# First layer of a two-layer streaming encoder: TensorE's order by a planner, and written out in pieces of three matmuls

## The chip, the cores and the metric

One core of one Trainium2 chip runs the whole program in one launch. The metric is device microseconds from the first to the last instruction of one execution; the median of three runs stands for a kernel. Engines are named as the profile names them: PE is TensorE (matmuls; PEld its weight loads), DVE VectorE, ACT ScalarE, POOL GpSimd, SP the engine that issues the transfers.

## The reference, cut to what matters

1024 prompt frames and 32 sample frames (T = 1056) of width 1024 go through two layers. The change lies in the first alone:

```python
def even_mixer(h, w_in, w_mix, scale, table, w_out, ...):
    proj = h @ w_in                              # 1024 -> 3072
    u, q, k, v, g_pool, g_att = split(proj)      # 512 columns each
    pool_out = multi_scale_pool(u, ...)          # 4 groups of 128, trailing means of 2, 4, 8, 16, minus u, times w_mix[g]
    att = band_attention(q, k, v, table)         # 8 heads of 64; own chunk of 64 frames and the 8 before, plus a bias
    mixed = concat([pool_out * silu(g_pool), att * silu(g_att)])
    return mixed @ w_out                         # then a norm and the residual
```

The 32 sample frames attend to 512 cached keys and values and to themselves. Layer two is an mLSTM with the same kind of projections.

## The kernel before, in words

**Layout.** Activations lie feature-major, tokens along the free axis, in three token groups (384, 384, 288: `GR`). A projection of 128 output columns ("a dense") reads one weight tile of 8 blocks of 128x128 and the normed input, both split into a high and a low part, so each block costs three matmuls (`mm3`, L106 to L108). One dense is 3 groups x 8 blocks x 3 = 72 matmuls. Each group goes to one of three PSUM buffers `pd` and is then evacuated by an `ev` function: by ACT for v (L248), by DVE for q and k (L256, L258), u (L612) and the gates (`gated`, L268 to L271, with a tanh on ACT between).

**Weights.** `take` hands out the weight tile that is asked for and loads the next one: a DMA, two casts on ACT (L93, tile `wh`), two subtractions on POOL (L94, tile `wl`). `wh` and `wl` have two buffers, so the next tile is split while the present one is multiplied, and its split can start only when the tile before is through.

**Layer 0** (`layer0`) works on four pairs of heads. The order in which the program is traced for each pair is: what was left of the fills; the transposes of v to token-major (`v_tokens`, L288 with ACT's L289 behind them); splits of q; the dense of k; its splits (`stacked`, `swapped`); the bias band B (DMA, a memset on POOL); the dense of the attention's gate, written into the tile `ga`, of which there is one; then the attention. `PLAN` names the denses put behind each pair (v and q of the next pair, u and gp of a pooling group): 4, 3, 3 and 4 of them, as fills.

**Attention.** A pair has two heads e and two halves hf of the 512 queries. `att_s(e, hf)` does the scores (L342, L343; 4 key blocks for hf 0, 8 for hf 1) in PSUM buffers `ps` (three), adds the bias (DVE L347, ACT L355), takes the maximum over the keys (DVE L363 to L371, then one `partition_all_reduce` on POOL, L373), subtracts it (DVE L377) and takes the exponential (ACT L378). `att_pv(e, hf)` multiplies by the values (L388, fp32, two instructions a block) into the one buffer `pv`, and `att_take` copies the result out (ACT L396, L397). `att_out` multiplies by the gate on POOL (L408), takes a reciprocal on DVE (L409) and stores to the DRAM tile `mix`. `att_sample` does the same for the 32 sample frames: its scores (L429, L430), an all-reduce of its own (L441), its exponential (L444), its values (L454) and a transpose (L459) in one function `rest`.

**Pooling.** `pool_sums` adds a group's windows on POOL (L477, one to four additions) and finishes on DVE (L481, L483); `pool_mix` multiplies by the mixing matrix (L495, one PSUM buffer `pm`) and by the gate gp (DVE L497).

**What sets the order.** The kernel is traced under Tile with `schedule_with_timeline_sim=True`: a planner runs a timing model over the traced program and, on each engine, places the instruction that is ready, earliest traced first. All engines then run their own list in order. So PE's list, too, is the planner's. After the four pairs, `out_proj` reads `mix` back in 384-token slices (`xr`, two buffers), splits them (ACT L195; POOL or DVE L196) into the tiles that the input had, and starts the output projection.

Of the kernel before, what the change touches and what calls it, by code (L numbers as in the profile page):

```python
# [15 lines left out]
DEC = 32  # L16
# [17 lines left out]
class Net:  # L34
# [36 lines left out]
    # keeps [s, t] with s <= t  # L71
# [4 lines left out]
    # ---------------------------------------------------------------- dense  # L76
# [40 lines left out]
    # the same, one token group at a time, to be put between other work; "make" gives evac when the tile starts  # L117
    def later(self, take, xs, make, after=None):
        box = {}

        def step(gi):
            if gi == 0:
                box["w"] = take()
                box["ev"] = make()
# [3 lines left out]
        self.fills += [lambda gi=gi: step(gi) for gi in range(3)]  # L128
# [15 lines left out]
    # r = 1/sqrt(sum/1024 + eps), on all partitions, from per-partition sums; worked out with the tokens on the partitions  # L144
# [44 lines left out]
    # split x * g into two parts of 12 bits  # L189
# [15 lines left out]
    # the input: one group's tokens, with tiles that are not in use yet for what comes in  # L205
# [23 lines left out]
    # ---------------------------------------------------------------- layer 0  # L229
# [32 lines left out]
    # (1 + tanh(g/2)) * g, twice the silu  # L262
# [11 lines left out]
    def v_tokens(self, vT, pr):  # L274
# [8 lines left out]
        for b0 in (0, 4, 8):  # L283
# [6 lines left out]
        for e in range(2):  # L290
            c0 = pr * 128 + e * 64
            cs = slice(e * 128, e * 128 + 64)
            nc.sync.dma_start(out=io["vo"][0:512, c0:c0 + 64].rearrange("(b p) c -> p b c", p=128), in_=vt[:, 4:8, cs])
            nc.sync.dma_start(out=io["vo"][512:544, c0:c0 + 64], in_=vt[:DEC, 8, cs])
        return vt

    # hi and lo of both heads, stacked on the partitions
# [21 lines left out]

    def att_s(self, pr, e, hf, Q, KA, KB, B):  # L320
# [7 lines left out]
        for group in banks:  # L328
            st = self.lp.tile([128, 1280], F32, name="st", bufs=4)
            tiles.append((st, [j for js in group for j in js]))  # L330
            off = 0
            for js in group:
# [28 lines left out]
        mx = self.lp.tile([128, 512], F32, name="mx", bufs=2)  # L361
        if hf == 0:
            nc.vector.tensor_copy(out=mx[:, 0:128], in_=place[0][0][:, 0:128])  # L363
            nc.vector.tensor_tensor(out=mx[:, 128:512], in0=place[0][0][:, 128:512], in1=place[1][0], op=ALU.max)
            rest = [2, 3]
        else:
            nc.vector.tensor_tensor(out=mx, in0=place[3][0], in1=place[4][0], op=ALU.max)
            rest = [2, 1, 0, 5, 6, 7]
        for j in rest:
            dst, a, b = place[j]  # L370
            nc.vector.tensor_tensor(out=mx[:, a - q0:b - q0], in0=mx[:, a - q0:b - q0], in1=dst, op=ALU.max)  # L371
        mb = self.lp.tile([128, 512], F32, name="mb", bufs=1)
        nc.gpsimd.partition_all_reduce(mb, mx, 128, bass_isa.ReduceOp.max)  # L373
        for st, js in tiles:
            for j in js:
                dst, a, b = place[j]
                nc.vector.tensor_tensor(out=dst, in0=dst, in1=mb[:, a - q0:b - q0], op=ALU.subtract)  # L377
            nc.scalar.activation(out=st, in_=st, func=AF.Exp)  # L378
        return place
# [12 lines left out]
    # values and sums of a head, from one tile to two: values on the head's partitions, sums beside them  # L392
# [21 lines left out]
    def att_sample(self, pr, qT, kT, vt, B, gate):  # L414
# [10 lines left out]
        def rest():  # L425
# [19 lines left out]
            # token-major  # L445
# [3 lines left out]
            for e in range(2):  # L449
# [7 lines left out]
                nc.vector.tensor_scalar(out=o[:, e], in0=pv[:, e, v0:v0 + 64], scalar1=rec[:, e:e + 1], scalar2=None, op0=ALU.mult)  # L457
            p = self.ps.tile([128, 512], F32, name="ps")
# [4 lines left out]
        return rest  # L463
# [22 lines left out]
    def pool_mix(self, g, u, gate):  # L486
# [3 lines left out]
        for s, n in GR:  # L490
# [7 lines left out]
            if g != 0:  # L498
                nc.sync.dma_start(out=self.mix[128 * g:128 * g + 128, s:s + n], in_=mo)

    def layer0(self):
# [85 lines left out]
        def do_v(pr):  # L587
            def make():
                rows["v", pr] = self.row()
                return self.plain(rows["v", pr])  # L590
            self.later(lambda: take(Vc + pr), xs, make)

        def do_q(pr):
            def make():
                rows["q", pr] = self.row()
                return self.scaled(rows["q", pr], 0.125)
            self.later(lambda: take(Qc + pr), xs, make)

        def do_u(g):
# [20 lines left out]
            self.later(lambda: take(U + g), xs, make, after)  # L620

        def do_gp(g):
# [3 lines left out]
            self.later(lambda: take(GP + g), xs, make, lambda: self.pool_mix(g, pools["u", g], pools["gp", g]))  # L626

        for pr in range(NPAIR):
            self.fill_all()
            vt = self.v_tokens(rows["v", pr], pr)  # L630
            qT = rows["q", pr]
            Q = self.stacked(qT, "qa")
            kT = self.row()
            self.dense(take(Kc + pr), xs, self.scaled(kT))
            nc.sync.dma_start(out=io["ko"][128 * pr:128 * pr + 128], in_=kT[:, 512:T])
            KA = self.stacked(kT, "ka")
            KB = self.swapped(KA, "kb")
            B = self.lp.tile([128, 2, 256], F32, name="B", bufs=1)
            for e in range(2):
                src = self.ext[2 * pr + e, 0:1, 128:129]  # L640
                nc.sync.dma_start(out=B[:, e], in_=bass.AP(tensor=src.tensor, offset=src.offset, ap=[[383, 128], [1, 256]]))
            nc.gpsimd.memset(B[64:128, :, 0:64], NEG)
            gate = self.lp.tile([128, T], F32, name="ga", bufs=1)
            samp = self.att_sample(pr, qT, kT, vt, B, gate)
            self.dense(take(GA + pr), xs, self.gated(gate))
            for f, g in PLAN[pr]:
                dict(u=do_u, gp=do_gp, v=do_v, q=do_q)[f](g)

            def S(e, hf):
                return self.att_s(pr, e, hf, Q, KA, KB, B)  # L650
            p00 = S(0, 0)
            p01 = S(1, 0)
            od = self.att_new()
            self.att_pv(0, 0, p00, vt, od)
            p10 = S(0, 1)
            samp()
            self.att_pv(1, 0, p01, vt, od)
            self.att_out(pr, od, 0, 512, gate)
            p11 = S(1, 1)
            od = self.att_new()  # L660
            self.att_pv(0, 1, p10, vt, od)
            self.att_pv(1, 1, p11, vt, od)
            self.att_out(pr, od, 512, 1024, gate)
        yield
        self.fill_all()
# [3 lines left out]
    # ---------------------------------------------------------------- out projection, norm, residual  # L669
    # the last rows of the input are still in self.late; returns what is left to do for the last tokens  # L670
# [76 lines left out]
    # the last tokens, with nothing left to hide behind  # L747
# [14 lines left out]
    # ---------------------------------------------------------------- layer 1  # L762
# [24 lines left out]
    def gates(self, gr):  # L787
        nc, io, lp = self.nc, self.io, self.lp
        # token-major
# [13 lines left out]
        # log sigmoid(f) = min(f, 0) - log(1 + exp(-|f|)), the log as 2 atanh(e / (2 + e))  # L803
# [12 lines left out]
        # b: running sums of lf in each chunk; c = ig - b  # L816
# [20 lines left out]
        # running maxima  # L837
# [27 lines left out]
        # exp(-m) by token  # L865
# [11 lines left out]
    # token-major, in one tile or split in two  # L877
# [115 lines left out]
    # h = num / max(|den|, exp(-m)), then its layer norm and the gates  # L993
# [230 lines left out]
```

## Time and profile before

| | us |
|---|---|
| three runs, median | 1272.95 |
| lowest and highest | 1272.43 and 1275.31 |
| span of the profiled execution | 1273.6 |
| PE busy in it | 1200.1 |
| DVE, ACT, POOL busy | 688.7, 471.5, 316.3 |

The page of the profile gives the span alone for the profiled execution; no other time of it is on it. It lies 0.65 us above the median of the runs. A row of a group of instructions has their busy time, the mean of one, and the idle time of the engine ahead of them with what ended it. A row of the timeline begins with the start and the duration in us, and ends, in brackets, with the idle time before it and what ended that.

### The profile page before, as it was taken

How to read it: one execution, taken by the hardware profiler on the slowest of the kernel's cores; microseconds unless marked ns; L12 is line 12 of the kernel's file. 1: busy time of each engine (PE TensorE's matmuls, PEld its weight loads, DVE VectorE, ACT ScalarE, POOL GpSimd, SP SyncE). 2: the span in 40 equal slices, each digit the busy share in tenths (PEclk: the TensorE clock that was granted, in tenths of full speed). 3: DMA queues.
4: the chain of work that ended last, by engine and by line, in shares of the span. 5: the costliest groups of instructions: out<-in, count | busy, mean ns of one | idle time of the engine just before them, and what ended most of it. 6: DMA issues, size and time to landing. Idle time of an engine off the chain costs nothing.

```text
span 1273.6 us, 19526 instructions
## 1 busy us (share of the span) xinstructions
PE 1200.1 (94%) x7457; PEld 1148.3 (90%) x7457; DVE 688.7 (54%) x1457; ACT 471.5 (37%) x976; POOL 316.3 (25%) x409
## 2 busy tenths in 40 slices
PE   6998898978997979999999999999999999999996
PEld 6997797977897859999999989999999999998996
DVE  7654474564676644777435643574237532567324
ACT  6532333243443335543033423343224322346421
POOL 3222532342234223552010320021002210123232
PEclk9998988989999989999999989999999999999998
DMA  6311120111120225332111132113111311113323
GB/s 216 114 38 33 44 85 26 51 59 34 64 71 22 78 85 168 100 127 83 49 51 53 37 71 97 38 49 95 46 50 51 76 68 50 42 60 122 127 99 124
DMA packets 79613, 94.03 MB, mean 74 GB/s; under 512 B 19208, under 2 KB 56856, under 8 KB 79520
## 3 DMA queue, kind: packets, MB, share of 16 engines
q1 hardware_dynamic: 79520, 92.79, 23.5%
q8 instruction: 58, 0.95, 0.3%
q14 instruction: 35, 0.29, 0.1%
HBM read 72.64 MB, written 21.69 MB: 74 GB/s over the span
## 4 chain that ended last, share of the span: by engine, by line
PE 77%; DVE 6%; issue 5%; DMA 5%; POOL 3%; ACT 2%; SPq 0%; DVEq 0%; POOLq 0%; ACTq 0%
PE pd L107 20%; PE pd L106 20%; PE pd L108 20%; PE pv L388 3%; DMA xr<-mix 2%; PE pm L883 1%; PE ps L951 1%; PE ps L343 1%; PE ps L342 1%; POOL qT L477 1%; DMA wr<-in_w0o 1%; POOL wl L94 1%; PE pv L918 1%; DMA MA<-mdr 1%; PE pv L920 1%
## 5 line engine op out<-in xcount | busy, mean ns | idle before, releaser
L106 PE MATMUL pd<-xh,wh 128*128 128x384 f32 (+1 forms) x1864 | 613.6, 330 | 13.5 <-DVE ga L268 6.8
L107 PE MATMUL pd<-xl,wh 128*128 128x384 f32 (+1 forms) x1864 | 612.8, 329 | 13.9 <-POOL xl L196 9.5
L108 PE MATMUL pd<-xh,wl 128*128 128x384 f32 (+1 forms) x1864 | 612.7, 329 | 1.7 <-DVE wl L94 1.6
L107 PEld LDWEIGHTS pd<-xl,wh 128*128 128x128 f32 x1864 | 356.1, 191 | 19.1 <-POOL xl L196 10.2
L106 PEld LDWEIGHTS pd<-xh,wh 128*128 128x128 f32 x1864 | 356.2, 191 | 18.2 <-ACT wh L93 7.6
L108 PEld LDWEIGHTS pd<-xh,wl 128*128 128x128 f32 x1864 | 356.0, 191 | 5.2 <-DVE wl L94 3.0
L93 ACT CAST wh<-wr 128x512 fp32r<-128x512 f32 x158 | 91.4, 618 | 149.6 <-PE pd L107 122.4
L94 DVE TENSOR_TENSOR wl<-wr,wh 128x512 fp32r<-128x512 f32 x116 | 80.5, 718 | 23.7 <-ACT wh L93 22.1
L94 POOL TENSOR_TENSOR wl<-wr,wh 128x512 fp32r<-128x512 f32 x42 | 57.8, 1392 | 116.8 <-ACT wh L93 59.6
L187 POOL TENSOR_TENSOR acc<-acc,sqt 128x384 f32<-128x384 f32 (+1 forms) x48 | 56.6, 1178 | 92.2 <-ACT sqt L186 87.8
L388 PE MATMUL pv<-st,vt 128*128 128x512 f32 (+1 forms) x192 | 58.7, 448 | 0.2 <-ACT st L378 0.2
L73 POOL TENSOR_SCALAR_AFFINE_SELECT D<-D 128x128 f32<-128x128 f32 (+1 forms) x36 | 11.9, 331 | 180.8 <-ACT D L947 168.1
L388 PEld LDWEIGHTS pv<-st,vt 128*128 128x128 f32 x192 | 36.2, 195 | 20.7 <-issue 12.4
L963 POOL TENSOR_TENSOR qa<-qT,MA 128x128 f32<-128x128 f32 (+1 forms) x64 | 27.1, 441 | 107.1 <-DMA MA<-mdr 68.4
L965 POOL TENSOR_TENSOR qal<-qa,qah 128x256 fp32r<-128x256 f32 (+1 forms) x32 | 27.0, 847 | 103.9 <-ACT qah L964 91.6
L347 DVE TENSOR_TENSOR st<-ps,B 128x256 f32<-128x256 f32 (+1 forms) x72 | 26.1, 377 | 45.0 <-PE ps L343 44.4
L377 DVE TENSOR_TENSOR st<-st,mb 128x512 f32<-128x512 f32 (+1 forms) x96 | 40.0, 485 | 15.7 <-POOL mb L373 14.1
L256 DVE TENSOR_TENSOR row<-pd,r 128x384 f32<-128x384 f32 (+1 forms) x36 | 18.6, 521 | 54.4 <-PE pd L108 54.2
L983 DVE SCALAR_TENSOR_TENSOR C<-C,MA,ps 128x258 f32<-128x258 f32 x64 | 30.4, 478 | 32.2 <-PE ps L920 19.0
L373 POOL PARTITION_ALL_REDUCE mb<-mx x16 | 28.8, 1799 | 66.5 <-issue 25.2
L378 ACT ACTIVATE st<-st 128x1280 f32<-128x1280 f32 x24 | 30.4, 1272 | 31.2 <-DVE st L377 31.1
L355 ACT ACTIVATE st<-ps,far 128x256 f32<-128x256 f32 (+3 forms) x56 | 25.6, 487 | 38.9 <-DVE st L347 35.8
(306 smaller groups left out, 1675.8 us busy)
## 6 DMA issues: line engine op xcount, KB each, us to landing
wr<-in_w SPq DMA_DIRECT2D x128, 256.0 KB, 2.7
xr<-mix SPq DMA_DIRECT2D x26, 192.0 KB, 2.9
wr<-in_w0o SPq DMA_DIRECT2D x16, 256.0 KB, 3.1
MA<-mdr SPq DMA_DIRECT2D x32, 128.0 KB, 3.2
wr<-in_w1o SPq DMA_DIRECT2D x16, 256.0 KB, 3.2
x<-in_x SPq DMA_DIRECT2D x16, 192.0 KB, 2.8
x<-x1d SPq DMA_DIRECT2D x16, 192.0 KB, 3.8
out_y<-y SPq DMA_DIRECT2D x16, 192.0 KB, 2.1
```

Of the source, the lines that this page charges most:

```text
L93: nc.scalar.copy(out=wh[:, k], in_=wr)
L94: eng.tensor_tensor(out=wl[:, k], in0=wr, in1=wh[:, k].bitcast(F32), op=ALU.subtract)
L106: nc.tensor.matmul(out=p, lhsT=wh[:, k], rhs=xh[:, k], start=first and i == 0, stop=False)
L107: nc.tensor.matmul(out=p, lhsT=wh[:, k], rhs=xl[:, k], start=False, stop=False)
L108: nc.tensor.matmul(out=p, lhsT=wl[:, k], rhs=xh[:, k], start=False, stop=last and i == len(ks) - 1)
L187: (eng or nc.gpsimd).tensor_tensor(out=acc, in0=acc, in1=t[:, :n], op=ALU.add)
L373: nc.gpsimd.partition_all_reduce(mb, mx, 128, bass_isa.ReduceOp.max)
L377: nc.vector.tensor_tensor(out=dst, in0=dst, in1=mb[:, a - q0:b - q0], op=ALU.subtract)
L378: nc.scalar.activation(out=st, in_=st, func=AF.Exp)
L388: nc.tensor.matmul(out=pv[:, a - q0:b - q0], lhsT=vt[:, j, 64 * e:64 * e + 128], rhs=dst, start=(i == 0), stop=(i == len(order) - 1))
L963: nc.gpsimd.tensor_tensor(out=qa[:, d, :L], in0=qT[:, d, t], in1=Ab, op=ALU.mult)
L983: nc.vector.scalar_tensor_tensor(out=Cn[:, d], in0=C[:, d], scalar=Ab[:, L - 1:L], in1=pu, op0=ALU.mult, op1=ALU.add)
```

## The change: what it does

PE's list for layer 0 is no longer the planner's. The whole loop over the pairs stands in `manual_schedule(engines={PE})`, so PE runs in the order traced; the other engines are still planned. The fills are cut into pieces of one block, three matmuls (`fine=True`): 24 pieces a dense. `along` issues the pieces one by one and puts an event between them when its number has come; `self.due` holds calls that come so many pieces later.

For each pair, `pair` writes out: 24 pieces of k, with the values of the pair before, head 0, second half, at piece 8; 24 pieces of the attention's gate, with the sample's scores at 10, the values of the pair before, head 1, second half (and `att_out`) at 14, v's transposes at 17 and 20; then the 96 or 72 pieces of `PLAN`, with the rest of v's transposes at 4, the scores in steps two pieces apart from 1, 8, 16 and 54 (46 in the last pair), the values of the first half at 42 and 50 (36 and 44), the sample's values at 62 and its transpose at 67, and in the last pair the values of the second half at 72 and 95. The mixing matmuls of the pooling come 20, 24 and 28 pieces after their gate (6, 10, 14 for group 1, at once for group 0). `att_s`, `att_sample`, `v_tokens` and `pool_mix` return their parts as calls instead of running through; their instructions are the same.

```diff
-    def later(self, take, xs, make, after=None):
+    def later(self, take, xs, make, after=None, fine=False):
...
+        def piece(gi, k):
+            s, n = GR[gi]
+            if k == 0:
+                if gi == 0:
+                    begin()
+                box["p"] = self.pd.tile([128, 512], F32, name="pd")
+            self.mm3(box["p"][:, :n], box["w"], xs[gi], [k], k == 0, k == 7)
+            if k == 7:
+                box["ev"](gi, s, n, box["p"])
+                if gi == 2 and after is not None:
+                    after()
+        if fine:
+            self.fills += [lambda gi=gi, k=k: piece(gi, k) for gi in range(3) for k in range(8)]
...
+    def along(self, events, n=999):
+        events = sorted(events, key=lambda e: e[0])
+        i = 0
+        while i < n and self.fills:
+            while events and events[0][0] <= i:
+                events.pop(0)[1]()
+            self.fill()
+            i += 1
+            for d in self.due:
+                d[0] -= 1
+            while self.due and self.due[0][0] < 0:
+                self.due.pop(0)[1]()
+        for e in events:
+            e[1]()
...
+    def pair(self, pr, take, xs, rows, do, before, Kc, GA):
...
+        qT = rows["q", pr]
+        Q = self.stacked(qT, "qa")
+        self.later(lambda: take(Kc + pr), xs, make_k, fine=True)
+        self.along([(8, f) for f in before[:1]])
+        kT = box["kT"]
...
+        self.later(lambda: take(GA + pr), xs, make_ga, fine=True)
+        ev = [(14, f) for f in before[1:]]
...
+        s_scores, s_values = self.att_sample(pr, qT, kT, box, B)
+        ev += [(10, s_scores), (17, values), (20, lambda: box["turn"](4))]
+        self.along(ev)
+        gate, vt = box["gate"], box["vt"]
+        for f, g in PLAN[pr]:
+            do[f](g)
+        end = pr == NPAIR - 1
+        place, ev = {}, []
+
+        for e, hf, at in ((0, 0, 1), (1, 0, 8), (0, 1, 16), (1, 1, 46 if end else 54)):
+            place[e, hf], steps = self.att_s(pr, e, hf, Q, KA, KB, B)
+            ev += [(at + 2 * i, f) for i, f in enumerate(steps)]
+        ev.append((4, lambda: box["turn"](8)))
...
+        ev += [(36 if end else 42, lambda: pv(0, 0)), (44 if end else 50, lambda: pv(1, 0))]
+        ev += [(62 + 5 * i, f) for i, f in enumerate(s_values)]
+        if end:
+            ev += [(72, lambda: pv(0, 1)), (95, lambda: pv(1, 1))]
+        self.along(ev)
+        return [lambda: pv(0, 1), lambda: pv(1, 1)]
...
+            self.later(lambda: take(GP + g), xs, make,
+                       lambda: self.due.extend([(0, 6, 20, 20)[g] + 4 * i * (g > 0), f] for i, f in
+                                               enumerate(self.pool_mix(g, pools["u", g], pools["gp", g]))), True)
...
+        with tc.manual_schedule(engines={mybir.EngineType.PE}):
+            for pr in range(NPAIR):
+                last = self.pair(pr, take, xs, rows, do, last, Kc, GA)
+            while self.due:
+                self.due.pop(0)[1]()
         yield
-        self.fill_all()
```

## Rows read from the trace of the kernel before

**Rows 1.** The page: its first line and PE's busy time.
```profile
span 1273.6 us, 19526 instructions
...
PE 1200.1 (94%) x7457; PEld 1148.3 (90%) x7457; DVE 688.7 (54%) x1457; ACT 471.5 (37%) x976; POOL 316.3 (25%) x409
```

**Rows 2.** Waits of PE, whole run: total us, times, longest.
```profile
PE pv L454 <- ACT ss L444: 20.4, 4, 6.1
PE pd L107 <- POOL xl L196: 9.5, 1, 9.5
PE pd L106 <- DVE ga L268: 6.8, 1, 6.8
...
PE pm L495 <- DVE u L483: 6.5, 2, 5.5
```

**Rows 3.** Stretches (us): busy PE, PEld, DVE, ACT, POOL; granted clock; DMA share; GB/s.
```profile
44.00:461.00 417.00, 373.54 (x2148) 343.91 (x2147) 245.38 (x476) 151.54 (x264) 128.53 (x128) 0.94 0.17 51
...
101.10:107.90 6.80, 6.34 (x29) 6.00 (x30) 3.10 (x10) 1.84 (x5) 1.78 (x1) 0.50 0.00 0
159.10:166.00 6.90, 5.32 (x19) 4.70 (x20) 5.63 (x7) 0.23 (x1) 2.65 (x3) 0.51 0.19 51
213.70:220.60 6.90, 5.82 (x27) 5.48 (x28) 5.67 (x18) 1.37 (x3) 1.78 (x1) 0.51 0.01 2
275.20:282.00 6.80, 4.04 (x13) 4.04 (x14) 6.80 (x11) 3.23 (x8) 2.50 (x2) 0.50 0.12 44
312.70:319.60 6.90, 4.99 (x24) 4.64 (x25) 3.68 (x14) 1.49 (x3) 2.28 (x2) 0.51 0.01 2
408.30:415.10 6.80, 3.77 (x18) 3.43 (x19) 5.43 (x14) 3.03 (x5) 2.33 (x2) 0.50 0.01 2
456.10:466.30 10.20, 5.96 (x14) 4.12 (x14) 3.30 (x6) 2.83 (x5) 2.98 (x3) 0.50 0.47 135
```

**Rows 4.** Timeline of PE, first piece behind the gate of the third pair.
```profile
277.96 0.69 PE L106 MATMUL pd<-xh,wh 128*128 128x384 f32 x1 [6.82 <-DVE ga L268]
```

**Rows 5.** Timeline of PE: pieces of a dense, sample scores, values of a second half.
```profile
83.32 0.34 PE L106 MATMUL pd<-xh,wh 128*128 128x384 f32 x1
...
85.40 0.33 PE L106 MATMUL pd<-xh,wh 128*128 128x384 f32 x1
...
88.50 1.00 PE L429 MATMUL ps<-qd,ck 128*128 128x64 f32 x8
...
259.39 4.47 PE L388 MATMUL pv<-st,vt 128*128 128x512 f32 x16
```

**Rows 6.** Timeline of POOL, first pair, either side of an all-reduce.
```profile
83.41 0.26 POOL L359 MEMSET st<- 64x64 f32 x2
90.57 2.53 POOL L94 TENSOR_TENSOR wl<-wr,wh 128x512 fp32r<-128x512 f32 x2 [6.91 <-ACT ss L435]
93.05 0.14 POOL L419 MEMSET qd<- 128x64 f32 x1
99.60 0.54 POOL L441 PARTITION_ALL_REDUCE smb<-sm  x1 [6.41 <-issue]
```

**Rows 7.** Timeline of DVE: the last step ahead of the sample's all-reduce.
```profile
90.76 0.74 DVE L440 TENSOR_REDUCE sm<-ss 128x64 f32<-128x320 f32 x1
```

**Rows 8.** The page's groups: busy us, mean ns, idle before and its releaser.
```profile
L93 ACT CAST wh<-wr 128x512 fp32r<-128x512 f32 x158 | 91.4, 618 | 149.6 <-PE pd L107 122.4
...
L94 POOL TENSOR_TENSOR wl<-wr,wh 128x512 fp32r<-128x512 f32 x42 | 57.8, 1392 | 116.8 <-ACT wh L93 59.6
...
L377 DVE TENSOR_TENSOR st<-st,mb 128x512 f32<-128x512 f32 (+1 forms) x96 | 40.0, 485 | 15.7 <-POOL mb L373 14.1
```

**Rows 9.** Groups of POOL in 44 to 461 us, shapes apart.
```profile
L408 POOL TENSOR_TENSOR ro<-ro,ga 128x512 f32<-128x512 f32 x7 | 10.4, 1489 | 15.9 <-ACT ro L396 15.9
...
L277 POOL MEMSET vt<- 128x832 f32 x3 | 2.4, 786 | 0.0
```

**Rows 10.** The tile ga: min, median and max ns of its first DVE operation.
```profile
L268 DVE TENSOR_TENSOR ga<-pd,r x12: 451/520/558, 61.9 to 373.0; 128x384 f32<-128x384 f32 x8, 128x288 f32<-128x288 f32 x4
```

More of the change, by code (lines that the diff above doesn't have):

```diff
@@ L115, in dense, with begin @@
             evac(gi, s, n, p)
-    def later(self, take, xs, make, after=None):
+    def later(self, take, xs, make, after=None, fine=False):
         box = {}
+        def begin():
+            box["w"] = take()
+            box["ev"] = make()
         def step(gi):
             if gi == 0:
-                box["w"] = take()
-                box["ev"] = make()
+                begin()
             self.dense(box["w"], xs, box["ev"], (gi,))
@@ L127, in step @@
                 after()
-        self.fills += [lambda gi=gi: step(gi) for gi in range(3)]
+        def piece(gi, k):
+            s, n = GR[gi]
+            if k == 0:
+                if gi == 0:
+                    begin()
+                box["p"] = self.pd.tile([128, 512], F32, name="pd")
[6 more added lines that the diff above has]
+            self.fills += [lambda gi=gi, k=k: piece(gi, k) for gi in range(3) for k in range(8)]
+        else:
+            self.fills += [lambda gi=gi: step(gi) for gi in range(3)]
     def fill(self, n=1):
@@ L282, in v_tokens, with turn @@
         v4 = vt.rearrange("p b (t c) -> p b t c", c=64)
-        for b0 in (0, 4, 8):
+        def turn(b0):
             p = self.pv.tile([128, 512], F32, name="pv") if b0 == 4 else self.pm.tile([128, 512], F32, name="pm")
@@ L289, in v_tokens @@
                 nc.scalar.mul(out=v4[:L, b, 0::2, :], in_=q.rearrange("p (t c) -> p t c", c=64), mul=self.rcol[:L, b:b + 1])
[L290 to L295, printed above, removed]
+            if b0 == 8:
+                for e in range(2):
+                    c0 = pr * 128 + e * 64
+                    cs = slice(e * 128, e * 128 + 64)
+                    nc.sync.dma_start(out=io["vo"][0:512, c0:c0 + 64].rearrange("(b p) c -> p b c", p=128), in_=vt[:, 4:8, cs])
+                    nc.sync.dma_start(out=io["vo"][512:544, c0:c0 + 64], in_=vt[:DEC, 8, cs])
+        return vt, turn
     def stacked(self, src, nm):
@@ L327, in att_s, with scores @@
         banks = (((0,), (1, 3), (2,)),) if hf == 0 else (((0, 2), (3,), (1,)), ((4,), (5, 7), (6,)))
[L328 to L332, printed above, removed]
+        off = 0
+        def scores(group, i):
+            nonlocal off
+            if i == 0:
+                tiles.append((self.lp.tile([128, 1280], F32, name="st", bufs=4), [j for js in group for j in js]))
+                off = 0
+            st = tiles[-1][0]
+            for js in group[i:i + 1]:
                 p = self.ps.tile([128, 512], F32, name="ps")
@@ L360, in att_s @@
                 off += w
[L361 to L371, printed above, removed]
@@ L381, in att_pv, with step @@
+        def step(b, i):
+            scores(banks[b], i)
+            if b == len(banks) - 1 and i == 2:
+                soft()
+        return place, [lambda b=b, i=i: step(b, i) for b in range(len(banks)) for i in range(3)]
     def att_pv(self, e, hf, place, vt, od):
@@ L412, in att_out, with att_sample @@
         nc.sync.dma_start(out=self.mix[r0:r0 + 128, q0:q1], in_=o[:, :n])
-    def att_sample(self, pr, qT, kT, vt, B, gate):
+    def att_sample(self, pr, qT, kT, own, B):
         nc, io = self.nc, self.io
@@ L423, in att_sample, with scores @@
             nc.vector.tensor_copy(out=qd[64 * e:64 * e + 64, e], in_=qT[64 * e:64 * e + 64, SEQ:T])
-        def rest():
+        box = {}
+        def scores():
             p = self.ps.tile([128, 512], F32, name="ps")
@@ L444, in rest, with values @@
             nc.scalar.activation(out=ss, in_=ss, func=AF.Exp)
+            box["ss"] = ss
+        def values():
+            ss, vt = box["ss"], own["vt"]
             o = self.lp.tile([DEC, 2, 64], F32, name="so", bufs=1)
@@ L457, in rest, with turn @@
                 nc.vector.tensor_scalar(out=o[:, e], in0=pv[:, e, v0:v0 + 64], scalar1=rec[:, e:e + 1], scalar2=None, op0=ALU.mult)
+            box["o"] = o
+        def turn():
+            o, gate = box["o"], own["gate"]
             p = self.ps.tile([128, 512], F32, name="ps")
@@ L462, in rest @@
             nc.sync.dma_start(out=self.mix[512 + 128 * pr:640 + 128 * pr, SEQ:T], in_=mo)
-        return rest
+        return scores, (values, turn)
     def pool_sums(self, g, u):
@@ L489, in pool_mix, with piece @@
         nc.sync.dma_start(out=wm, in_=io["wmix"][g])
-        for s, n in GR:
+        def piece(s, n):
             p = self.pm.tile([128, 512], F32, name="pm")
@@ L499, in pool_mix @@
                 nc.sync.dma_start(out=self.mix[128 * g:128 * g + 128, s:s + n], in_=mo)
+        return [lambda s=s, n=n: piece(s, n) for s, n in GR]
+    def along(self, events, n=999):
[12 more added lines that the diff above has]
+            e[1]()
@@ new lines, in pair, with make_k, make_ga, values @@
+    def pair(self, pr, take, xs, rows, do, before, Kc, GA):
+        nc = self.nc
+        box = {}
+        def make_k():
+            box["kT"] = self.row()
+            return self.scaled(box["kT"])
+        def make_ga():
+            box["gate"] = self.lp.tile([128, T], F32, name="ga", bufs=1)
+            return self.gated(box["gate"])
+        qT = rows["q", pr]
[3 more added lines that the diff above has]
+        kT = box["kT"]
+        nc.sync.dma_start(out=self.io["ko"][128 * pr:128 * pr + 128], in_=kT[:, 512:T])
+        KA = self.stacked(kT, "ka")
+        KB = self.swapped(KA, "kb")
+        B = self.lp.tile([128, 2, 256], F32, name="B", bufs=1)
+        for e in range(2):
+            src = self.ext[2 * pr + e, 0:1, 128:129]
+            nc.sync.dma_start(out=B[:, e], in_=bass.AP(tensor=src.tensor, offset=src.offset, ap=[[383, 128], [1, 256]]))
+        nc.gpsimd.memset(B[64:128, :, 0:64], NEG)
+        self.later(lambda: take(GA + pr), xs, make_ga, fine=True)
+        ev = [(14, f) for f in before[1:]]
+        def values():
+            box["vt"], turn = self.v_tokens(rows["v", pr], pr)
+            box["turn"] = turn
+            turn(0)
+        s_scores, s_values = self.att_sample(pr, qT, kT, box, B)
[10 more added lines that the diff above has]
+        ev.append((4, lambda: box["turn"](8)))
+        od = {}
+        def pv(e, hf):
+            if e == 0:
+                od[hf] = self.att_new()
+            self.att_pv(e, hf, place[e, hf], vt, od[hf])
+            if e == 1:
+                self.att_out(pr, od[hf], 512 * hf, 512 * hf + 512, gate)
+        ev += [(36 if end else 42, lambda: pv(0, 0)), (44 if end else 50, lambda: pv(1, 0))]
[4 more added lines that the diff above has]
+        return [lambda: pv(0, 1), lambda: pv(1, 1)]
@@ L590, in make @@
                 return self.plain(rows["v", pr])
-            self.later(lambda: take(Vc + pr), xs, make)
+            self.later(lambda: take(Vc + pr), xs, make, fine=True)
         def do_q(pr):
@@ L596, in make @@
                 return self.scaled(rows["q", pr], 0.125)
-            self.later(lambda: take(Qc + pr), xs, make)
+            self.later(lambda: take(Qc + pr), xs, make, fine=True)
         def do_u(g):
@@ L619, in after @@
                 self.pool_sums(g, u)
-            self.later(lambda: take(U + g), xs, make, after)
+            self.later(lambda: take(U + g), xs, make, after, True)
         def do_gp(g):
@@ L625, in make @@
                 return self.gated(pools["gp", g])
-            self.later(lambda: take(GP + g), xs, make, lambda: self.pool_mix(g, pools["u", g], pools["gp", g]))
-        for pr in range(NPAIR):
-            self.fill_all()
[L630 to L663, printed above, removed]
@@ L664, in layer0 @@
         yield
-        self.fill_all()
         self.late = {0: pools["gp", 0]}
```

28 lines of the change are left out of this document (21 added, 7 removed).

## The prediction

> **What bounds the kernel now.** I read the page first: PE is busy for 1200 of 1274 us [rows 1], so what a new order of its list can bring is what PE loses to idling and to its clock. The view of waits, for PE alone, says where it idles: 20.4 us in four waits for the sample's exponential, 9.5 for one split of the output projection's input, 6.8 for a gate, 6.5 in two waits for the pooling's DVE work [rows 2]. All lie in the stretch from 44 to 461 us, the four pairs and the step to the output projection, whose mean granted clock is 0.94 [rows 3]. [...] Idle and clock make 43.2 + 18.2 = 61.4 us. That is all that the change can win; the other side is what its own waits cost.
>
> **The machine behind those waits** is POOL. Its timeline shows a gap of 6.9 us between a memset and the next subtraction, though all-reduces and memsets had just followed each other closely, and 6.4 us between a memset and the next all-reduce whose data DVE had finished at 91.5 us, eight us before it began [rows 6, 7]. I read this as a switch: POOL pays 6.4 us to go over to an all-reduce and 6.9 to come back to an ordinary operation, and the time runs from the end of the instruction ahead, a memset included. [...]
>
> **The change, part by part.** Its work is the same: same matmuls, same DVE, ACT and POOL instructions, same transfers. What moves is when.
>
> *Sample* (removed wait). Before, its values stood soon behind its scores, and PE waited for two POOL switches. After, 14 pieces of the gate and 62 of the fills lie between. Four pieces of 384 tokens take 2.08 us [rows 5], so a piece takes 0.52, one of 288 tokens 0.39 by columns, a dense 16 x 0.52 + 8 x 0.39 = 11.4. 76 pieces are over 35 us; the longest of the four waits was 6.1 [rows 2]. All 20.4 us go, with the clock behind them: 3.2 + 2.9 + 2.5 + 1.9 = 10.5. Together **-30.9**.
>
> *Pooling matmuls*: moved 20 to 28 pieces, some 10 us, behind their gate (group 1 by 6, with a whole dense of gp ahead of that). The longest such wait was 5.5 us. **-9.2** (6.5 and 2.7).
>
> *The old wait for a gate* [rows 4]: 6.8 + 2.0 = **-8.8**.
>
> *Step to the output projection*: before, the last all-reduce stood among the splits and POOL paid both switches there. After, the last scores are 40 pieces earlier, so POOL is back at ordinary work. -12.5, less what stays: the three mixing matmuls of group 0 come last, one behind the other through the single `pm` buffer, and the input's splits can start only when gp 0's first group is through, 16 pieces (some 7 us) before the end. Not shown before; between 0 and the old 12.5 I take 4, for one or two short waits. **-8.5**.
>
> *New wait for the gate* (pairs 1 to 3). `att_out` of the pair before now stands behind piece 14 of the new gate's dense, and the new gate can't be written before it: there is one `ga`. The three `pd` buffers hold the gate's three groups, so PE can go through the dense, but then stops. Count from its first piece. POOL: the next weights, two casts of 0.62 on ACT and two subtractions of 1.39 [rows 8], end at 4.0; switch, 10.4; the sample's all-reduce (0.54), whose scores were issued at 5.2, 10.9; the memset of `vt` waits for the values of head 1, which start at 14 x 0.52 + 1.0 = 8.3 and take 4.5 [rows 5], and takes 0.79 [rows 9], 13.6; switch, 20.5; multiplication 1.5 [rows 9], 22.0; DVE's first gate operation 0.52 [rows 10], 22.5. PE: 11.4 + 1.0 + 4.5, and eight transposes at 0.22 (by the columns of the values) 1.8: 18.7. PE waits 3.8 us, three times, and by the mean of rows 3 (18.2 / 7) 2.6 each for the clock: **+19.2**. If POOL multiplies before the all-reduce, it ends by 15 and the wait is 0; with a pooling sum in front it could be the 6.8 of rows 4 each time, 3 x 9.4 = 28.2.
>
> *DVE held behind an all-reduce.* DVE's list is still the planner's. If it puts a subtraction of the maximum ahead of bias additions, and POOL is late by a switch, the three `ps` buffers stay full and PE stops. Before, DVE idled 14.1 us for this reason [rows 8] with no PE wait of its own in rows 2. Scores now come in steps of two pieces, some 1.4 us with their matmuls, so three buffers cover 4 us. Between 0 and 14.1 I take **+3**, near the end that the waits show.
>
> *Weights behind an all-reduce.* A subtraction can start only when the tile before is through and must end within a dense, 11.4 us. Casts 1.2, switch 6.9, first half 1.4: 9.5. It fits, unless the all-reduce is still to run: the second half of head 1 ends at piece 64 and the next tile of weights in the first pair comes at 72, so the all-reduce can be some 4 us late there. **+2**, between 0 and 4 x 2.6 + 4 = 14.4 if every pair pays.
>
> *At nothing*: v's transposes (moved behind k; k's row then has to take q's buffer, free once q is split, and the splits of q are over before k's first group ends); the queue of SP (v's cached rows, v's stores and the mixing weights are issued a dense later, and 40 pieces or more lie before their readers); values of the first half (37 to 42 pieces, over 19 us, behind their scores). If a switch and an all-reduce of 8.7 us, or two, come late there, these still hold.
>
> **The sum**: -30.9 - 9.2 - 8.8 - 8.5 + 19.2 + 3 + 2 = -33.2. The profiled execution spans 1273.6, which is 0.65 above the median of the runs, less than a measurement of this kernel can tell (about 0.2%, 2.5 us). 1273.6 - 33.2 = 1240.4, **1240**.
>
> **Rivals.**
> *The gate is in time.* POOL's list has the multiplication ahead of the sample's all-reduce, or less work in front. For it: before, only one of the pairs waited for a gate [rows 2], though `ga` was single then too. Against: the scores stand four pieces earlier in the trace, so the planner sees their all-reduce ready first. It gives 1240.4 - 19.2 = 1221.
>
> *POOL becomes the bound* (slower). The spread scores set each of a pair's five all-reduces between ordinary operations: ten switches, 5 x (6.4 + 6.9) = 66.5 us, and POOL's busy 128.5 / 4 = 32 [rows 3]: 99 us for a pair that had 417 / 4 = 104. From 5 us of waiting for data per pair on, POOL is slower than the old kernel. With 10 us, four pairs take 436, 19 more than before; the clock behind one more stop per pair adds 10; the output projection's step gives back 8.5: 1294. Against it: scores of the first half lie seven pieces apart and should share a switch, so eight is likelier than ten.
>
> *The waits change places.* What the sample loses, weights and gate take: new waits at their upper bounds, 28.2 + 14.1 + 14.4 = 56.7, against 57.4 won: 1273.
>
> *The order does nothing.* Were PE's list already as good as POOL allows, the manual one would give the same time; rows 2 speak against it, as 20.4 us have one cause that distance cures.
>
> **How the numbers follow.** The forecast, with its waits between near 0 and 1.5 times what I took, 1228 to 1252, has 0.48. The gate in time, 1214 to 1228, 0.26. Heavier waits, still faster, 1252 to 1270, 0.12. No difference (the waits change places, or the order does nothing) 0.04. POOL as the bound, slower, 0.10. The range for 8 in 10 takes the first two and part of the third: its low end is all 61.4 won with 2 left (1214), its high end 1264. Faster 0.86, within 0.2% 0.04, slower 0.10.
>
> **What would show it.** In the waits of PE after: no wait for the sample's exponential and none of over 1 us for the pooling's DVE work. At the end of the gate's dense in pairs 1 to 3, PE waits for DVE's L268 some 4 us, with POOL's row of all-reduce, memset, gap of 7 us and multiplication just before. In the windows: three or four stretches at 0.50 in layer 0 where there were seven. The step to the output projection has no POOL gap of 7 us. I am wrong if PE shows waits for weights (ACT or POOL, L93, L94) of 5 us in several pairs, if POOL shows four switches a pair more than before, or if PE waits for `ps` over 5 us per pair.

## The result, and the profile after

The changed kernel takes 1326.59 us (median of 4 runs, 1322.96 to 1328.22) against 1273.55 for the kernel before: ratio 1.0414, 95% interval 1.0396 to 1.0432, 53 us slower. The forecast was 1240, range 1214 to 1264; the result lies outside, on the side that had a chance of 0.10. The first lines of the page answer to [rows 1]:

```profile
span 1323.8 us, 19544 instructions
...
PE 1221.6 (92%) x7457; PEld 1157.5 (87%) x7457; DVE 680.2 (51%) x1457; ACT 475.2 (36%) x976; POOL 309.0 (23%) x409
```

The waits of PE in the stretch from 44 to 520 us, the four pairs and the start of the output projection, against [rows 2] (line numbers have moved: L308 are v's transposes with ACT's L309 behind them, L369 the scores, L422 the values, L494 the sample's values):

```profile
PE ps L369 <- DVE st L374: 15.0, 16, 2.8
PE pv L308 <- ACT vt L309: 14.7, 12, 5.3
PE pv L422 <- ACT rg L431: 14.5, 3, 5.4
PE pm L308 <- ACT vt L309: 13.0, 12, 4.6
PE pv L494 <- DVE so L497: 7.0, 4, 3.7
PE ps L369 <- ACT st L382: 5.8, 1, 5.8
PE pd L108 <- POOL wl L94: 0.8, 1, 0.8
```

None of the old causes is there as a wait of its own: no sample's exponential, no gate, no pooling, no split of the output projection's input. In their place PE waits 70.0 us for readers of PSUM, where all its waits in layer 0 were 43.2 before: for ACT to copy v out, for DVE and ACT to take scores, for ACT to copy the values out, for DVE to take the sample's values. The clock follows; the stretches at 0.50 in 44 to 520 us (columns as in [rows 3]):

```profile
69.10:75.90 6.80, 3.80 (x13) 2.79 (x13) 1.79 (x7) 2.40 (x7) 0.21 (x1) 0.50 0.00 0
188.60:202.20 13.60, 9.35 (x33) 7.85 (x34) 5.73 (x8) 4.72 (x12) 2.44 (x2) 0.50 0.14 39
239.80:246.60 6.80, 5.21 (x11) 3.40 (x12) 1.63 (x3) 4.05 (x7) 3.48 (x2) 0.50 0.12 39
297.80:311.40 13.60, 9.28 (x33) 7.78 (x34) 5.53 (x7) 4.87 (x12) 2.36 (x2) 0.50 0.14 39
349.00:355.80 6.80, 5.88 (x13) 4.06 (x14) 1.41 (x1) 4.00 (x7) 4.02 (x3) 0.50 0.16 46
413.80:420.60 6.80, 5.59 (x20) 5.11 (x21) 1.88 (x4) 2.92 (x7) 1.22 (x1) 0.50 0.27 77
461.60:468.40 6.80, 4.28 (x11) 3.48 (x12) 6.27 (x5) 4.74 (x8) 3.73 (x5) 0.50 0.00 2
482.10:488.90 6.80, 5.00 (x23) 4.66 (x24) 2.73 (x8) 2.54 (x2) 0.00 (x0) 0.50 0.00 0
...
120.30:123.70 3.40, 3.40 (x9) 1.99 (x7) 1.41 (x1) 1.46 (x2) 2.83 (x2) 0.50 0.13 41
471.90:475.30 3.40, 3.40 (x13) 3.40 (x13) 2.13 (x7) 0.37 (x1) 0.00 (x0) 0.50 0.38 121
```

Half of PE's busy time in them, my estimate of what the clock took, is 27.6 us, against 18.2; the timelines show a little less than half: a matmul of 384 columns starts 0.32 us behind the one ahead of it at 0.50 (before, 106.68 to 107.32 us) and 0.17 at full clock (12 in 2.08 us, [rows 5]). Over the whole execution, the two spans differ by 50.2 us: PE's idle time (the span less its busy time) by 28.7, the clock (by that estimate, half of the busy time in all stretches at 0.50) by 14.3, 37.0 against 22.7; the other 7.2 are PE time that the profile counts as busy. Where much of the idle time lies shows in the timeline of PE, at the first pair's transposes:

```profile
66.11 0.27 PE L308 MATMUL pm<-ident,row 128*128 128x128 f32 x1
70.98 0.48 PE L308 MATMUL pm<-ident,row 128*128 128x128 f32 x1 [4.60 <-ACT vt L309]
71.92 0.48 PE L308 MATMUL pm<-ident,row 128*128 128x128 f32 x1 [0.46 <-ACT vt L309]
...
76.16 0.33 PE L308 MATMUL pv<-ident,row 128*128 128x128 f32 x1 [0.46 <-ACT vt L309]
76.95 0.33 PE L308 MATMUL pv<-ident,row 128*128 128x128 f32 x1 [0.46 <-ACT vt L309]
```

Four transposes write one PSUM buffer, and each waits until ACT has read the one before: 0.46 us idle, and 0.33 in which the transpose runs alone, 0.79 from start to start at full clock (76.16 to 76.95). The 4.60 us are of another kind: ACT came late, as theory B below has it. In the kernel before, the planner had put other pieces between; its timeline has

```profile
47.82 0.33 PE L288 MATMUL pv<-ident,row 128*128 128x128 f32 x1
47.91 0.42 PE L108 MATMUL pd<-xh,wl 128*128 128x384 f32 x1
48.16 0.33 PE L106 MATMUL pd<-xh,wh 128*128 128x384 f32 x1
```

so a transpose and the piece's matmul behind it took 0.34 from start to start. Such a matmul alone takes 0.17 (12 of them 2.08, [rows 5]), which leaves some 0.17 for the transpose there. In the changed kernel the transpose at 76.95 starts behind ACT's copy of the one ahead of it, which runs from 76.53 to 76.90.

### The profile page after: what moved, and what is told of

Read it like the earlier page. It is cut to its first block, busy times and chain, and to the rows that moved or that the text cites. A ratio compares the mean times of both kernels' runs of the same rounds, so it can differ in the third digit from the quotient of the medians.

```text
span 1323.8 us, 19544 instructions
## 1 busy us (share of the span) xinstructions
PE 1221.6 (92%) x7457; PEld 1157.5 (87%) x7457; DVE 680.2 (51%) x1457; ACT 475.2 (36%) x976; POOL 309.0 (23%) x409
## 4 chain that ended last, share of the span: by engine, by line
PE 61%; DVE 6%; DMA 4%; ACT 2%; issue 2%; POOL 1%; SPq 0%; DVEq 0%; ACTq 0%; POOLq 0%
PE pd L106 16%; PE pd L107 16%; PE pd L108 16%; PE pv L422 2%; DMA wr<-in_w0o 2%; DMA xr<-mix 1%; PE pm L977 1%; PE ps L1045 1%; PE pv L1012 1%; DVE st L406 1%; DMA MA<-mdr 1%; PE pv L1014 1%; PE pv L1013 1%; PE ps L1012 1%; DVE wl L94 1%
## 5 line engine op out<-in xcount | busy, mean ns | idle before, releaser
L94 DVE TENSOR_TENSOR wl<-wr,wh 128x512 fp32r<-128x512 f32 x116 | 80.6, 719 | 27.5 <-ACT wh L93 25.7
L94 POOL TENSOR_TENSOR wl<-wr,wh 128x512 fp32r<-128x512 f32 x42 | 57.0, 1373 | 114.5 <-ACT wh L93 66.3
L422 PE MATMUL pv<-st,vt 128*128 128x512 f32 (+1 forms) x192 | 60.8, 471 | 14.5 <-ACT rg L431 14.5
L206 POOL TENSOR_TENSOR acc<-acc,sqt 128x384 f32<-128x384 f32 (+1 forms) x48 | 52.5, 1093 | 86.2 <-ACT sqt L205 85.8
L422 PEld LDWEIGHTS pv<-st,vt 128*128 128x128 f32 x192 | 37.5, 206 | 37.4 <-ACT rg L431 15.4
L369 PE MATMUL ps<-qa,kb 128*128 128x512 f32 (+1 forms) x96 | 33.0, 349 | 20.8 <-DVE st L374 15.0
```

Of the source, the lines that this page charges most:

```text
L94: eng.tensor_tensor(out=wl[:, k], in0=wr, in1=wh[:, k].bitcast(F32), op=ALU.subtract)
L206: (eng or nc.gpsimd).tensor_tensor(out=acc, in0=acc, in1=t[:, :n], op=ALU.add)
L369: nc.tensor.matmul(out=p[:, w:w + n], lhsT=KB[e][:, ks], rhs=Q[e][:, a:b], start=True, stop=False)
L422: nc.tensor.matmul(out=pv[:, a - q0:b - q0], lhsT=vt[:, j, 64 * e:64 * e + 128], rhs=dst, start=(i == 0), stop=(i == len(order) - 1))
```

## The experiments

Theory A, the buffer: written out by hand, two writers of one PSUM buffer follow each other (four transposes, two key blocks of one score buffer, the two heads of the sample), and the second waits for the first one's reader. Theory B, the late queue: POOL starts all-reduces a switch late; the subtraction on DVE and the exponential on ACT wait at the head of their lists, and what PE needs stands behind them. One chain of B in the changed kernel, timelines of POOL, DVE, ACT and PE:

```profile
112.20 1.80 POOL L402 PARTITION_ALL_REDUCE mb<-mx  x1 [5.95 <-PE pv L422]
...
114.04 2.30 DVE L406 TENSOR_TENSOR st<-st,mb 128x128 f32<-128x128 f32 x5 [8.72 <-POOL mb L402]
...
115.83 1.27 ACT L407 ACTIVATE st<-st 128x1280 f32<-128x1280 f32 x1 [14.73 <-DVE st L406]
...
118.62 0.56 ACT L430 COPY ro<-pv 64x512 f32<-64x512 f32 x1
119.19 0.58 ACT L431 COPY rg<-pv 64x512 f32<-64x512 f32 x1
...
119.83 0.79 PE L422 MATMUL pv<-st,vt 128*128 128x512 f32 x1 [4.55 <-ACT rg L431]
```

The copies at 118.62 take values of head 0 that PE had finished at 111.8; they stand behind exponentials of another half, which wait for the all-reduce. The gate reaches PE in the same way. Timelines of ACT and PE, second pair:

```profile
194.89 0.99 ACT L289 ACTIVATE th<-ga 128x384 f32<-128x384 f32 x2 [1.90 <-DVE ga L287]
195.78 0.35 ACT L309 ACTIVATE vt<-pv,rcol 128x128 f32<-128x128 f32 x1
...
196.19 0.47 PE L308 MATMUL pv<-ident,row 128*128 128x128 f32 x1 [2.67 <-ACT vt L309]
```

ACT's copy of v stands behind the tanh of the gate, which waits for DVE and, through it, for POOL's late multiplication. Pairs 2, 3 and 4 each have one such wait on a transpose (2.67, 2.59 and 5.30 us), 9.2 us beyond the usual 0.46.

**1. PE's order back to the planner** (1282.6 us, ratio 1.0055, 1.003 to 1.0079)

```diff
-        with tc.manual_schedule(engines={mybir.EngineType.PE}):
+        with nullcontext():
```

> The changed kernel with PE's order given back to the planner (pieces, events and traced order stay). Theory A (one PSUM buffer): written by hand, two writers of one PSUM buffer follow each other, and the second waits until the first one's part is read out; the planner puts other pieces between. Then PE's waits on the readers of v's transposes, score pairs and sample values (49.7 us in the changed kernel) fall under 10 us and the time is 1250 to 1285 us. Theory B (late queues): PE waits because ACT and DVE are held behind all-reduces that POOL starts a switch late, whoever orders PE; then 1305 us or more.

44 us of the 53 go, by that line alone; with it the planner also writes the other engines' lists anew, as in every run here. The longest of PE's waits, in an execution of 1287.72 us:

```profile
PE pd L106 <- DVE ga L287: 15.0, 3, 5.3
```

Waits on transposes, score pairs and the sample's heads are down to some 3 us in all, as A has it; 23.7 us are new, the sample's scores (9.8) and the pooling (13.9). The wait for the gate, L287, is the one I had forecast.

**2. Spread: one piece between two writers of a buffer** (1288.43 us, 1.0102, 1.008 to 1.0124)

```diff
-        ev += [(10, s_scores), (17, values), (20, lambda: box["turn"](4))]
+        ev += [(10, s_scores), (17, values), (20, lambda: box["turn"](4, 0))]
+        ev += [(17 + i, lambda i=i: box["turn"](0, i)) for i in (1, 2, 3)]
+        ev += [(20 + i, lambda i=i: box["turn"](4, i)) for i in (1, 2, 3)]
...
-            ev += [(at + 2 * i, f) for i, f in enumerate(steps)]
+            ev += [(at + i, f) for i, f in steps]
...
-        ev += [(62 + 5 * i, f) for i, f in enumerate(s_values)]
+        ev += [(62 + i, f) for i, f in s_values]
```

> The changed kernel, PE's order still by hand, with one piece between two writers of the same PSUM buffer: v's transposes one by one at pieces 17 to 23, the second key block of a score buffer one piece later, the sample's second head three pieces after its first. Theory A: the 49.7 us of those waits fall under 20 and the time to 1275 to 1300 us. Theory B: the short waits of some 0.5 us go, about 15 us in all at most, the long ones of 2 to 5 us stay, 1308 to 1320 us.

```profile
PE ps L376 <- DVE st L381: 13.1, 6, 2.7
PE ps L376 <- ACT st L391: 8.7, 4, 6.6
PE pd L106 <- DVE ga L287: 8.7, 3, 3.5
PE pm L312 <- ACT vt L313: 7.3, 3, 4.2
```

The order stays by hand, and 38 us go. The waits named fall from 49.7 to 20.4 (13.1 + 7.3), just over the 20 that A had allowed; the time is A's. What is left has other sizes, up to 6.6 us, behind DVE and ACT. The gate shows as a wait of its own now, three times, 2.9 us in the mean; in the changed kernel it cost about as much through the transposes. The 14.5 us behind L431 are gone as well, though POOL switches as before: at the place of the chain above, ACT now has the copies (104.98 us) ahead of the exponentials (110.99). So the 38 us are not A's alone.

**3 and 4. Without the all-reduce over the keys**, the changed kernel (1262.64 us, 0.9900, 0.9885 to 0.9915) and the kernel before (1233.11 us, 0.9666, 0.9652 to 0.9680)

```diff
-            mb = self.lp.tile([128, 512], F32, name="mb", bufs=1)
-            nc.gpsimd.partition_all_reduce(mb, mx, 128, bass_isa.ReduceOp.max)
+            mb = mx
...
-            mb = self.lp.tile([128, 2, DEC], F32, name="smb", bufs=1)
+            mb = m
```

> The changed kernel without the all-reduce over the keys: every partition subtracts its own maximum, in the scores and in the sample. POOL then has no switches. Theory A: the waits on one buffer's readers stay, over 30 us, and it stays 25 to 40 us above the kernel before treated the same way. Theory B: those two are within 10 us of each other, both under 1250 us.

> The kernel before without the all-reduce over the keys, as the run above. Both theories: the waits for the sample's exponential and the gate go, 1215 to 1240 us; it is the yardstick for the run above.

```profile
PE ps L369 <- DVE st L374: 13.8, 16, 1.5
PE pv L308 <- ACT vt L309: 6.4, 12, 0.8
PE pm L308 <- ACT vt L309: 5.6, 12, 0.6
...
PE pv L494 <- DVE so L497: 4.3, 4, 1.1
```

These are the changed kernel's waits with B taken out: the same counts (16, 12, 12, 4), none over 1.5 us, 30.1 us in all, and 29.5 us between the two kernels. So A is real by itself, and of the 49.7 us in the changed kernel some 20 were B's. The all-reduces, with the switches that they bring, cost the kernel before 42 us, most of what I had counted as winnable.

**5 and 6. Moving waits about in the spread kernel**: the sample's scores at piece 23 (1293.11 us, 1.0137, 1.0120 to 1.0154), then also the last scores six pieces later (1297.62 us, 1.0173, 1.0155 to 1.0190)

```diff
-        ev += [(10, s_scores), (17, values), ...
+        ev += [(23, s_scores), (17, values), ...
...
-        for e, hf, at in ((0, 0, 1), (1, 0, 8), (0, 1, 16), (1, 1, 46 if end else 54)):
+        for e, hf, at in ((0, 0, 1), (1, 0, 8), (0, 1, 16), (1, 1, 52 if end else 60)):
```

> The spread kernel (one piece between two writers of one PSUM buffer), with the sample's scores at piece 23 of the gate's dense and not at 10. Theory B (rest of the loss from queues held behind a late all-reduce): POOL then multiplies by the gate ahead of the sample's all-reduce and ACT copies v out ahead of the sample's exponential; the waits for the gate (8.7 us in the spread kernel) and on v's transposes (7.3) fall under 3 us each, time 1268 to 1282 us. Theory A alone (only the PSUM buffer matters): no change, within 3 us of the spread kernel's 1288.

> The kernel of the run above, with the scores of head 1, second half, six pieces later (60, in the last pair 52), behind DVE's 3.3 us reciprocal for the first half. Theory B: the waits of PE on the readers of the score buffers (13.1 and 8.7 us in the spread kernel) fall by at least 8 us, time 4 to 14 us under the run above. Theory A alone: within 3 us of it.

Neither came out. In run 5 the gate's wait went (8.7 to 0) and v's fell (7.3 to 1.9), as B has it, but the score buffers took it all back, 21.8 to 41.7:

```profile
PE ps L376 <- DVE st L381: 26.8, 12, 3.8
PE ps L376 <- ACT st L391: 14.9, 4, 6.5
```

In run 6 the score buffers fell to 24.7 and 16.2 us of waits for the mixing matmuls (L550) came up, which the spread kernel did not have. My reading is that a late all-reduce holds whatever stands behind it, and another order chooses what that is; these two runs fit it, but the times that it gave were not met.

**7 and 8. One part of the change alone, in the kernel before**: the sample's values five groups of fills later (1264.27 us, 0.9916, 0.9893 to 0.9938), then also the mixing matmuls behind the next gate (1284.55 us, 1.0073, 1.0052 to 1.0093)

```diff
+            if pr < NPAIR - 1:
+                self.fills.insert(5, late)
+            else:
+                self.fill(5)
+                late()
...
-            self.later(lambda: take(GP + g), xs, make, lambda: self.pool_mix(g, pools["u", g], pools["gp", g]))
+            def after():
+                pend.append(lambda: self.pool_mix(g, pools["u", g], pools["gp", g]))
+                if g < 2:
+                    pend.pop()()
+            self.later(lambda: take(GP + g), xs, make, after)
...
+            while pend:
+                pend.pop(0)()
```

> The kernel before, PE's order the planner's, with one part of the change alone: the sample's values and their transpose are traced five groups of the fills later. If the prediction's term for that part holds (-30.9 us), 1240 to 1255 us. If the wait only moves to what follows (the gate, the transposes of v, an all-reduce), 1262 to 1278 us.

> The run above, and the mixing matmuls of groups 3 and 2 traced behind the next pair's gate instead of in front of its transposes. If that term holds too (-9.2 us), 5 to 10 us under the run above; if the wait moves, within 3 us of it.

Run 7 shows what distance alone is worth. The wait for the sample's exponential is gone, and the exponential is not:

```profile
PE ps L342 <- ACT st L355: 16.7, 4, 5.8
PE pv L388 <- ACT st L378: 9.1, 3, 3.3
```

ACT still stands at it (its timeline has the exponential at 101.97 us after 10.77 us of idling for DVE), and the score buffers behind it now stop PE (rows of an execution of 1269.48 us, the longest of four). 11.7 us are won where I had forecast 31. The mixing matmuls do not wait any more in run 7 already; moving them as well, run 8, is 20 us worse, with score buffers at 24.9 and values at 15.5 us.

**9 to 12. Layer 0's ordinary work taken off POOL, with the work complete**: the split of layer 0's weights, the multiplication by the gate and the pooling's additions go to DVE; memsets and part of the output projection's splits stay on POOL

```diff
-        self.weng = nc.gpsimd
+        self.weng = nc.vector
...
-        nc.gpsimd.tensor_tensor(out=o[:, :n], in0=o[:, :n], in1=gate[:, q0:q1], op=ALU.mult)
+        nc.vector.tensor_tensor(out=o[:, :n], in0=o[:, :n], in1=gate[:, q0:q1], op=ALU.mult)
...
-            nc.gpsimd.tensor_tensor(out=dst[:, lo:L], in0=src[:, lo:L], in1=src[:, lo - sh:L - sh], op=ALU.add)
+            nc.vector.tensor_tensor(out=dst[:, lo:L], in0=src[:, lo:L], in1=src[:, lo - sh:L - sh], op=ALU.add)
```

> The kernel before with the ordinary work of layer 0 (split of the weights, multiplication by the gate, the pooling's additions) on DVE instead of POOL, so that POOL stays with all-reduces and memsets and need not switch. Theory B: the waits of PE for the sample's exponential (20.4), the gate (6.8) and the pooling (6.5) fall to under 12 us together, 1235 to 1258 us. Rival: DVE, with some 50 us more work, holds PE instead, 1266 us or more.

> The spread kernel (PE's order by hand, one piece between two writers of one PSUM buffer) with the same work moved to DVE. Theories A and B are both met then: waits on score buffers, gate and v's transposes (37.8 us in the spread kernel) fall under 15, 1240 to 1262 us. Rival (DVE full): 1275 us or more.

> The changed kernel with the same work moved to DVE and no spreading. Theory A: it stays 20 to 40 us above the run above, with the short waits of 0.46 us on v's transposes all there; theory B alone: within 8 us of the run above.

> The kernel before with the sample's values traced later and the same work moved to DVE. If late all-reduces were what the sample's wait moved to, it is 5 to 15 us under the run of the kernel before with the work moved alone, 1228 to 1250 us; if not, within 4 us of it.

Medians in us; the ratio is that of the third column. The kernel before ran at 1273.55 to 1276.85 beside these.

| | POOL as it was | layer 0's ordinary work on DVE | ratio to before, 95% |
|---|---|---|---|
| kernel before | 1276.85 | 1240.66 | 0.9718 (0.9685 to 0.9751) |
| changed kernel | 1326.59 | 1264.83 | 0.9923 (0.9892 to 0.9955) |
| changed, spread | 1288.43 | 1239.25 | 0.9714 (0.9685 to 0.9743) |
| before, sample later | 1264.27 | 1217.79 | 0.9551 (0.9516 to 0.9585) |

Runs 9 and 11 came out as B with A has it, and run 10 does but for 0.75 us below its range. The changed kernel treated so keeps A's waits, with their counts, and stays 25.6 us above the spread one:

```profile
PE ps L369 <- DVE st L374: 12.2, 16, 1.3
PE pm L308 <- ACT vt L309: 9.7, 12, 4.7
PE pv L308 <- ACT vt L309: 6.4, 12, 0.8
```

The spread one's score buffers wait 4.0 us instead of 21.8. Run 12 is 22.9 us under run 9, more than the 5 to 15 of its expectation, and not for the reason given there: run 9 has no wait for the sample's exponential left. Its longest wait is at the output projection, where its last all-reduce still stands among splits on POOL; waits of PE and timeline of POOL:

```profile
PE pd L107 <- POOL xl L196: 8.2, 1, 8.2
...
415.85 0.98 POOL L196 TENSOR_TENSOR xl<-xr,xh 128x384 fp32r<-128x384 f32 x1 [7.11 <-issue]
```

In run 12 the last all-reduce comes before these splits. It has no wait of PE over 1 us between 44 and 520 us; POOL's gaps ahead of two all-reduces of its first pair are 1 to 2 us:

```profile
93.53 0.52 POOL L443 PARTITION_ALL_REDUCE smb<-sm  x1 [2.22 <-DVE sm L442]
...
96.14 1.78 POOL L373 PARTITION_ALL_REDUCE mb<-mx  x1 [1.21 <-DVE mx L371]
```

It is 4.5% faster than the kernel before, the fastest of all runs here, with PE's order the planner's.

Run 9 took away a second thing as well. DVE's maximum (L371) takes 280 to 1966 ns in the kernel before, where the long ones run beside ordinary work on POOL (384 columns take 1.54 us at 134.15, during POOL's L94, and 0.56 at 85.90, while POOL idles), and 273 to 559 in run 9. Run 4 speaks against this as the cause of the gain: there the ordinary work stays on POOL and L371 takes up to 2243 ns, and it gains 42 us. What runs 4 and 9 both end is POOL's going back and forth in the four pairs.

## Why the prediction was wrong

*At nothing: v's transposes.* This is the step that failed most. I checked what the transposes' new place does to k's row and to the transfers, and in the gate's count I took them at 0.22 us each by their columns. I did not ask what PE does between a write into a PSUM buffer and the next write into the same one. Written by hand, PE has no other work there: 0.79 us for each instead of some 0.17. The planner's list of before had other pieces there, unasked. The sum had no term for it, nor for the score pairs and the sample's heads, which were tied in the same way. Spreading took off 38 us (run 2), 25.6 without POOL's part (runs 10 and 11), and the two kernels without all-reduces differ by 29.5 (runs 3 and 4): the term that stood at nothing was 25 to 30 us.

*Sample, -30.9.* The wait named went, the gain did not: run 7, that part alone, gives 11.7 us. I treated the wait as PE's own, ended by distance. It was a late all-reduce, and it holds ACT's list as well; score buffers and values behind it stop PE next. My rule that distance covers it looked only at who reads the exponential, not at what is queued behind it on ACT.

*DVE held behind an all-reduce, +3.* The mechanism was right and its size was not: in the spread kernel, where A is out, score buffers cost 21.8 us. I took the low end because the old kernel showed no such wait; runs 7 and 8 have it with the planner's order too, 17.1 and 24.9 us. The prediction's own sign of being wrong, over 5 us of waits for `ps` per pair, came out in the changed kernel: 20.8 us in four pairs.

*The clock behind a wait, 18.2 before and 2.6 for each new one.* That PE's work takes twice as long at a granted clock of 0.50 no run shows. The factor in the timelines is 1.85 (0.320 against 0.173 us from one matmul of 384 columns to the next), so of the 36.2 us of PE busy time in the seven stretches of [rows 3] some 16.6 were the clock's.

*Weights, +2*: 0.8 us of waits. *Pooling matmuls*: their wait is gone, as said, and it is gone in run 7 too, where they were not moved: it was one of those that trade places. *Output projection, -8.5*: PE has one wait of 0.6 us for a split there, as POOL had no all-reduce left among the splits.

*The gate, +19.2.* The count of POOL's steps held; its timeline in the changed kernel, second pair:

```profile
184.45 0.54 POOL L477 PARTITION_ALL_REDUCE smb<-sm  x1 [5.97 <-issue]
184.94 0.81 POOL L296 MEMSET vt<- 128x832 f32 x1
193.01 1.25 POOL L442 TENSOR_TENSOR ro<-ro,ga 128x512 f32<-128x512 f32 x1 [7.26 <-ACT vt L309]
```

All-reduce, memset, a switch of 7.3, multiplication: the order forecast. The cost came by a path that I had not seen, through ACT's list to the transposes, 9.2 us in the three pairs; in the spread kernel it comes as forecast, 2.9 us three times, against 3.8.

*The rivals.* "The waits change places" was the nearest, with 0.04 and the two kernels even; its mechanism shows in runs 5, 6 and 8, and it lacked A. "POOL becomes the bound" had the sign and the wrong cause: without any all-reduce the changed kernel is still 29.5 us behind.

These terms do not add up to the whole miss, as they were measured in different kernels. The 7.2 us of added busy time stay open. They are not the 44 hand-overs: busy time without the clock's part, taken as half, is 1177.4 us before, 1184.6 in the changed kernel and 1186.2 in the spread one, which has few hand-overs left.

## What to carry to other kernels

Before you write an engine's order by hand, list the pairs of its instructions that share a PSUM buffer with a reader between them, and put a piece of other work between every two. Ask of a wait not only who waits, but which instruction stands at the head of which queue and what is behind it: in run 7 distance moved most of such a wait, and in run 9 ending its cause removed it. An engine that pays for changing its kind of work, as POOL does here with mostly 5.8 to 7.8 us a change, should be given one kind, even where the other engine is busier; here that took 36 to 62 us off each of four kernels.

## What was not expected of the hardware

POOL pays the switch in both directions every time: in the changed kernel and in the spread one its idle time is mostly 5.8 to 6.5 us ahead of an all-reduce behind ordinary work, never less, and mostly 6.7 to 7.8 the other way, never less, 16 times each way in layer 0 of either kernel, with a memset between or not. That I had read from the trace; how much hangs on it I had not. With the ordinary work on DVE, which is then busy for 56% of the span instead of 54, the kernel before gains 36 us.
